# Where weight sums and weight staging stand among the reads of the product banks

## The chip, the core and the metric

The kernel runs on one core of a Trainium2 chip. The metric is the device time of one launch in microseconds (us). Three runs of the kernel before took 2848.87 to 2852.09 us, with a median of 2852.01 us.

## The reference, cut to what matters

The program is a small encoder trunk of two layers over 768 tokens (one request of 512, one of 256, weights shared), all in float32, model width 1024, inner width 2816:

```python
def swiglu_ffn(x, w1, w2):
    gate, up = jnp.split(x @ w1, 2, axis=-1)
    return (jax.nn.silu(gate) * up) @ w2
...
for li in range(DEPTH):
    x = x + 0.5 * swiglu_ffn(rmsnorm(x, norm_g[li, 0]), ffn_w1[li, 0], ffn_w2[li, 0])
    h = rmsnorm(x, norm_g[li, 1])
    ...  # layer 0: gated linear recurrence (HGRN2); layer 1: windowed attention
    x = x + mix
    x = x + 0.5 * swiglu_ffn(rmsnorm(x, norm_g[li, 2]), ffn_w1[li, 1], ffn_w2[li, 1])
return rmsnorm(x, final_norm_g)
```

There are four feed-forward networks (f0 to f3), and between them the HGRN2 mixer and the attention mixer. The change bears on the feed-forward networks above all.

## The kernel before

**Precision.** Each float32 operand is split into a rounded part ("hi", written by ScalarE as a cast to fp32r) and the rest ("lo", VectorE's subtraction). A product of two split operands is three matmuls: hi·hi, hi·lo, lo·hi.

**Seven products for eight.** The feed-forward products are cut into 2 by 2 blocks and done with a Winograd-style scheme of seven block products, p1 to p7, where some factors are sums of blocks. On the weights' side there are four sums: `s3` (a DRAM load to which GpSimd's DMA adds a block), `a21 += a22` (GpSimd's DMA adds one block to the other in SBUF), and two that VectorE forms: `a11 += a21` (call it the second sum; p6 reads it) and `a12 += a11` (the fourth sum; p3 reads it). p1 must read `a11` before the second sum overwrites it, and p2 must read `a12` before the fourth.

**One feed-forward network.** Its 22 inner blocks are worked in five groups g of four and a rest of two. For each inner block `up_pair` computes gate and up with seven products of twelve 128x384 matmuls (line 421), in the order p1 p7 p2 p5 p4 p6 p3, on four PSUM banks a to d; p2 is added onto the bank of p1, p4 onto that of p7, p3 onto that of p5, each after something has read the bank (lines 438 to 455). After four inner blocks `down_quad` multiplies the four hidden blocks by a 512x1024 piece of w2: seven products of eighteen 128x512 matmuls (line 479), in the order p1 p2 p5 p4 p7 p6 p3. Each product fills three banks (one for each block of 128 tokens), and VectorE reads each bank into the residual x with `add_x` (line 501). p2 goes onto the banks of p1, p4 onto those of p5, p3 onto those of p7, so a bank must have been read before the second of the pair writes to it. There are 20 such quads, five in each network. On TensorE the built order of a quad is p1, p2, p5, eight matmuls of p7, p4, the rest of p7, p6, p3.

**Staging of weights.** `load_next` issues a quad's raw loads on SyncE's queue into four `wr` buffers, and the DMAs that add blocks on GpSimd's. `quad_steps` gives one step for each product: `split` casts hi on ScalarE (line 199) and subtracts on VectorE (line 200; for p5 of an up pair on GpSimd), into eight `w` buffers. The steps p1 and p2 each add their sum right behind their split (lines 206 and 210). `done` frees a product's `w` buffers and calls `ahead`, which traces the next steps as far as buffers go. In the down quads a split covers 128x1024, in the up pairs 128x512.

**What sets the order.** The kernel is traced in Python, and a scheduler then sets each engine's instruction order from data dependences and priorities that follow the traced order. Each engine's queue runs strictly in the built order: an instruction that waits holds up all behind it. `keep_in_program_order` (new in the change) puts an instruction behind whatever was traced before it on its engine.

Of the kernel before, what the change touches and what calls it, by code (L numbers as in the profile page):

```python
# [23 lines left out]
NBLK = T // P  # L24
# [23 lines left out]
class Trunk:  # L48
# [123 lines left out]
    def quad_steps(self, key, raws, srcs, order):  # L172
        nc = self.nc
        flat = lambda t: t.rearrange("p a b -> p (a b)")
        up = len(raws) == 2
        if up:
            a11, a12, a21, a22 = (flat(t[:, h : h + 4, :]) for t in raws for h in (0, 4))
            three = [srcs[1].rearrange("(k p) c -> p k c", p=P)[:, :4, :]]
        else:
            a11, a12, a21, a22 = (flat(t) for t in raws)  # L180
            three = [srcs[2][:, i : i + 1, :] for i in range(2)]
        s3 = []
        for i, src in enumerate(three):
            t = self.wp.tile([P, 512], F32, tag="s3", name=self.name("s3"), bufs=2)
            self.last_load = nc.sync.dma_start(t.rearrange("p (a b) -> p a b", a=src.shape[1]), src)
            self.into(t, a11[:, i * 512 : (i + 1) * 512])
            s3.append(t)
        self.into(a21, a22)

        def split(name, srcs, eng=None):  # L190
            if up:
                w = self.wtile()
                hi, lo = w[:, :512], w[:, 512:]
            else:
                hi, lo = self.wtile(), self.wtile()
            n = srcs[0].shape[-1]
            for i, src in enumerate(srcs):
                h, l = (t[:, i * n : (i + 1) * n] for t in (hi, lo))
                nc.scalar.copy(h, src)  # L199
                (eng or nc.vector).tensor_sub(l, src, h.bitcast(F32))  # L200
            view = lambda t: t.rearrange("p (a b) -> p a b", a=4 if up else 2)
            self.staged[(*key, name)] = (view(hi), view(lo), 1 if up else 2)

        def p1():
            split("p1", [a11])
            nc.vector.tensor_add(a11, a11, a21)  # L206

        def p2():
            split("p2", [a12])
            nc.vector.tensor_add(a12, a12, a11)  # L210

        steps = {
            "p1": p1,
            "p2": p2,
            "p3": lambda: split("p3", [a12]),
            "p4": lambda: split("p4", [a22]),
            "p5": lambda: split("p5", [a21], nc.gpsimd if up else None),
            "p6": lambda: split("p6", [a11]),
            "p7": lambda: split("p7", s3),
        }  # L220
        return [(1 if up else 2, steps[name]) for name in order]

    def stage_next(self):
        if not self.loaded:
# [10 lines left out]
    def take(self, key):  # L235
        while key not in self.staged:
            self.stage_next()
        return self.staged[key][:2]

    def done(self, key):  # L240
        self.held -= self.staged.pop(key)[2]
        self.ahead()

    def ahead(self):
# [20 lines left out]
    def split(self, src, hi, lo):  # L265
        self.nc.scalar.copy(hi, src)  # L266
        self.nc.vector.tensor_sub(lo, src, hi.bitcast(F32))  # L267
# [148 lines left out]
    def product(self, key, name, src, ps, first, last):  # L416
        wh, wl = self.take((*key, name))
        for k in range(4):
            a, b = (wh[:, k, :], wl[:, k, :]), self.operand(src, k)
            for i, (x, y) in enumerate(((0, 0), (0, 1), (1, 0))):  # L420
                self.nc.tensor.matmul(  # L421
                    ps,
                    a[x],
                    b[y],
                    start=first and k == 0 and i == 0,
                    stop=k == 3 and i == 2,
                    skip_group_check=True,
                )
        self.done((*key, name))

    def up_pair(self, tag, j):
        nc = self.nc
        key = (tag, j)
        a, b, c, d = (self.ps(H) for _ in range(4))
        v, w, t = (self.tmp(H) for _ in range(3))
        p = lambda name, ps, first, last: self.product(key, name, FACTOR[name], ps, first, last)
        p("p1", a, True, False)
        nc.scalar.copy(v, a)
        p("p7", c, True, False)
        nc.scalar.copy(w, c)  # L440
        p("p2", a, False, True)
        nc.scalar.activation(a, a, AF.Silu)
        p("p5", d, True, False)
        nc.vector.tensor_sub(w, w, d)  # L444
        p("p4", c, False, True)
        p("p6", b, True, True)
        nc.vector.tensor_sub(v, v, b)
        nc.vector.tensor_sub(t, c, v)
        nc.vector.tensor_mul(t, t, a)  # L449
        yield t  # L450
        nc.vector.tensor_sub(w, w, v)
        p("p3", d, False, True)
        nc.vector.tensor_add(v, v, d)
        self.last_act = nc.scalar.activation(v, v, AF.Silu).ins
        self.last_dve = nc.vector.tensor_mul(w, v, w).ins
        yield w

    def down_quad(self, tag, g, hid):
        nc = self.nc
# [177 lines left out]
    def hgrn_proj(self, h, out):  # L637
        nc = self.nc
        qk = self.big([P, 2, T])
        qs, kd = qk[:, 0, :], qk[:, 1, :]  # L640
        f, q, k = (self.big([P, 2, T]) for _ in range(3))
        for c0, dst, func in ((0, qs, AF.Copy), (3, f[:, 1, :], AF.Sigmoid), (4, f[:, 0, :], AF.Sigmoid)):
            key = ("hgrn", h, c0)
            wh, wl = self.take(key)
            for s, (off, n) in enumerate(SEQS):
                ps = self.ps(n)
                for kk in range(NC):
                    b = tuple(self.h[kk][:, i, off : off + n] for i in range(2))
                    self.mm3(ps, (wh[:, kk, :], wl[:, kk, :]), b, kk == 0, kk == NC - 1)
                    if kk in ((1, 3, 5), (3,))[s]:  # L650
                        yield
                if s:
                    self.done(key)
                nc.scalar.activation(dst[:, off : off + n], ps, func)
                yield
        for d in range(2):
            fd, j = f[:, 1 - d, :], slice(h, h + 1)
            nc.vector.tensor_scalar(fd, fd, self.om_lb[:, d, j], self.lb[:, d, j], ALU.mult, ALU.add)
            nc.scalar.activation(k[:, d, :], fd, AF.Identity, bias=1.0, scale=-1.0)
            nc.vector.tensor_mul(q[:, 1 - d, :], qs, fd)  # L660
        nc.vector.tensor_add(kd, k[:, 0, :], k[:, 1, :])
        out.update(h=h, qs=qs, kd=kd, f=f, q=q, k=k)
# [340 lines left out]
    def out_proj(self, tag, half, act, next_row):  # L1003
        for c in range(2):
            for b in range(NBLK):
                ps = self.ps()
                sl = slice(b * P, (b + 1) * P)
                for i in range(4):
                    key = (tag, half, c, i // 2)
                    wh, wl = self.take(key)  # L1010
                    t = act[half * 4 + i]
                    self.mm3(ps, (t[:, 0, sl], t[:, 1, sl]), (wh[:, i % 2, :], wl[:, i % 2, :]), i == 0, i == 3)
                    if i % 2 and b == NBLK - 1:
                        self.done(key)
                    if i == 1:
                        yield
                self.add_x(self.x[b][:, c * 512 : (c + 1) * 512], ps, 1.0)
                if half and c:
                    self.after_block(b, next_row)
                    if b >= 4:  # L1020
                        self.run_later()
                elif not half and b % 2:
                    self.run_later()
                yield
# [257 lines left out]
```

## Time and profile before

| | |
|---|---|
| median of 3 runs | 2852.01 us |
| profiled execution | 2852.12 us, its span from first to last instruction 2850.3 us |
| TensorE clock granted | 0.998 |
| TensorE matmul busy | 2796.7 us, 98% of the span |
| VectorE busy | 2173.2 us, 76% |
| ScalarE busy | 1318.9 us, 46% |
| GpSimd busy | 355.1 us, 12% |
| DMA | mean 102 GB/s |

A row of the profile names the source line, the engine, the operation and the tiles as out<-in. PE is TensorE, DVE VectorE, ACT ScalarE, POOL GpSimd, SP SyncE. "Idle before" is how long the engine sat idle ahead of an instruction, and the arrow names what ended it. Matmuls are pipelined and their ends are modelled, so distances between starts say more than busy time.

### The profile page before, as it was taken

How to read it: one execution, taken by the hardware profiler on the slowest of the kernel's cores; microseconds unless marked ns; L12 is line 12 of the kernel's file. 1: busy time of each engine (PE TensorE's matmuls, PEld its weight loads, DVE VectorE, ACT ScalarE, POOL GpSimd, SP SyncE). 2: the span in 40 equal slices, each digit the busy share in tenths (PEclk: the TensorE clock that was granted, in tenths of full speed). 3: DMA queues.
4: the chain of work that ended last, by engine and by line, in shares of the span. 5: the costliest groups of instructions: out<-in, count | busy, mean ns of one | idle time of the engine just before them, and what ended most of it. 6: DMA issues, size and time to landing. Idle time of an engine off the chain costs nothing. (4 is left out here: it accounts for less than half of the span.)

```text
span 2850.3 us, 40558 instructions
## 1 busy us (share of the span) xinstructions
PE 2796.7 (98%) x15225; PEld 2554.2 (90%) x15225; DVE 2173.2 (76%) x3750; ACT 1318.9 (46%) x2454; POOL 355.1 (12%) x402
## 2 busy tenths in 40 slices
PE   8999999999999999999999999999999899999998
PEld 8899999889899889998998998999888789989997
DVE  7788787468577658878878887887848878788877
ACT  7344443434344336434444643444458755434443
POOL 1111111000000001111111111111002211111110
PEclk9999999999999999999999999999999999999999
DMA  6554454311111133555444355545422113555443
GB/s 165 127 125 122 116 134 121 115 44 39 44 39 38 60 97 86 132 127 122 123 119 114 84 134 127 122 121 124 126 71 75 37 51 90 135 126 125 117 121 96
DMA packets 330101, 291.37 MB, mean 102 GB/s; under 512 B 11608, under 2 KB 257840, under 8 KB 329904
## 3 DMA queue, kind: packets, MB, share of 16 engines
q1 hardware_dynamic: 294064, 212.43, 25.4%
q0 software_dynamic: 31680, 62.93, 12.6%
q10 hardware_dynamic: 4160, 13.42, 1.3%
q8 instruction: 119, 1.95, 0.3%
q14 instruction: 78, 0.64, 0.1%
HBM read 216.39 MB, written 9.44 MB: 79 GB/s over the span
## 5 line engine op out<-in xcount | busy, mean ns | idle before, releaser
L421 PE MATMUL ps<-big,w 128*128 128x384 f32 x6720 | 1172.8, 334 | 3.1 <-DVE tA L444 2.9
L421 PEld LDWEIGHTS ps<-big,w 128*128 128x128 f32 x6720 | 1165.4, 188 | 8.8 <-DVE tA L444 7.2
L199 ACT CAST w<-wr 128x512 fp32r<-128x512 f32 x600 | 416.1, 707 | 722.7 <-PE ps L421 321.0
L479 PE MATMUL ps<-w,big 128*128 128x512 f32 x2520 | 586.8, 391 | 17.4 <-DVE x L501 17.4
L479 PEld LDWEIGHTS ps<-w,big 128*128 128x128 f32 x2520 | 469.4, 188 | 129.7 <-DVE x L501 17.3
L200 DVE TENSOR_TENSOR w<-wr,w 128x512 fp32r<-128x512 f32 (+1 forms) x520 | 438.1, 853 | 95.7 <-ACT w L199 87.0
L501 DVE SCALAR_TENSOR_TENSOR x<-ps,x 128x512 f32<-128x512 f32 x468 | 305.5, 682 | 20.5 <-PE ps L479 10.2
L141 POOL DMA_DIRECT2D s<-wr x120 | 105.4, 878 | 1333.4 <-DMA wr<-in_ffn_w_dram 583.0
L261 PE MATMUL ps<-w,big 128*128 128x512 f32 x624 | 249.8, 400 | 0.2
L263 PE MATMUL ps<-w,big 128*128 128x512 f32 x624 | 245.2, 393 | 2.5 <-DVE big L330 1.3
L262 PE MATMUL ps<-w,big 128*128 128x512 f32 x624 | 244.4, 392 | 0.0
L266 ACT CAST big<-tA 128x384 fp32r<-128x384 f32 x296 | 148.0, 513 | 175.0 <-DVE tA L449 72.0
L261 PE MATMUL ps<-big,w 128*128 128x384 f32 (+2 forms) x640 | 220.8, 346 | 3.3 <-ACT big L266 2.0
L262 PE MATMUL ps<-big,w 128*128 128x384 f32 (+2 forms) x640 | 216.8, 339 | 0.7 <-DVE big L267 0.5
L263 PE MATMUL ps<-big,w 128*128 128x384 f32 (+2 forms) x640 | 215.7, 337 | 0.0
L167 DVE TENSOR_TENSOR w<-wr,w 128x1024 fp32r<-128x1024 f32 x92 | 111.6, 1222 | 83.6 <-ACT w L166 59.7
L141 POOL DMA_DIRECT2D wr<-wr x100 | 87.5, 875 | 680.0 <-DVE tA L350 319.8
L267 DVE TENSOR_TENSOR big<-tA,big 128x384 fp32r<-128x384 f32 x296 | 164.2, 566 | 7.9 <-ACT big L266 4.4
L206 DVE TENSOR_TENSOR wr<-wr,wr 128x512 f32<-128x512 f32 (+1 forms) x100 | 79.3, 793 | 114.5 <-DMA wr<-wr 85.9
L166 ACT CAST w<-wr 128x1024 fp32r<-128x1024 f32 x92 | 96.6, 1052 | 120.5 <-PE ps L262 99.7
L263 PEld LDWEIGHTS ps<-w,big 128*128 128x128 f32 x624 | 117.4, 188 | 28.8 <-DVE big L330 2.0
L261 PEld LDWEIGHTS ps<-w,big 128*128 128x128 f32 x624 | 117.8, 189 | 22.3 <-issue 0.6
(170 smaller groups left out, 3317.2 us busy)
## 6 DMA issues: line engine op xcount, KB each, us to landing
wr<-in_ffn_w_dram SPq DMA_DIRECT2D x264, 512.0 KB, 3.9
s<-in_ffn_w_dram SPq DMA_DIRECT2D x120, 256.0 KB, 3.0
s<-wr POOLq DMA_DIRECT2D x120, 256.0 KB, 4.0
wr<-wr POOLq DMA_DIRECT2D x80, 256.0 KB, 4.0
wr<-in_hg_w_in_dram SPq DMA_DIRECT2D x40, 512.0 KB, 3.8
wr<-wr POOLq DMA_DIRECT2D x20, 512.0 KB, 4.6
spill<-x ACTq DMA_DIRECT2D x12, 512.0 KB, 3.0
x<-spill ACTq DMA_DIRECT2D x12, 512.0 KB, 3.3
```

Source lines behind the costliest of these rows:

```text
L141: self.nc.gpsimd.dma_start(out, src, accum_op=ALU.add)
L167: self.nc.vector.tensor_sub(lo, raw, hi.bitcast(F32))
L199: nc.scalar.copy(h, src)
L200: (eng or nc.vector).tensor_sub(l, src, h.bitcast(F32))
L261: nc.tensor.matmul(out, a[0], b[0], start=first, stop=False)
L262: nc.tensor.matmul(out, a[0], b[1], start=False, stop=False)
L263: nc.tensor.matmul(out, a[1], b[0], start=False, stop=last)
L266: self.nc.scalar.copy(hi, src)
L267: self.nc.vector.tensor_sub(lo, src, hi.bitcast(F32))
L421: self.nc.tensor.matmul(ps, a[x], b[y], start=first and k == 0 and i == 0, stop=k == 3 and i == 2, skip_group_check=True,)
L479: nc.tensor.matmul(ps, a[x], w[y], start=name == chain and kp == 0 and q == 0, stop=kp == 1 and q == 2, skip_group_check=True,)
L501: self.nc.vector.scalar_tensor_tensor(x, ps, c, x, ALU.mult, ALU.add)
```

## The change

Three edits. First, the two VectorE sums of a weight quad leave the steps p1 and p2. In a down quad the second sum is traced right in front of the split of p6 and the fourth in front of that of p3; in an up pair the second sum follows the split of p5 and the fourth that of p4. Each is pinned behind what was traced before it on VectorE. Second, `product` no longer stages: it only releases its buffers, and `up_pair` calls `ahead` after the instruction that reads the product's bank. Third, in `hgrn_proj` and `out_proj` the call of `done` moves behind the read of the bank. No instruction is added or taken away but one activation-table load less on ScalarE.

```diff
@@ quad_steps
-        def p1():
-            split("p1", [a11])
-            nc.vector.tensor_add(a11, a11, a21)
-
-        def p2():
-            split("p2", [a12])
-            nc.vector.tensor_add(a12, a12, a11)
-
-        steps = {
-            "p1": p1,
-            "p2": p2,
-            "p3": lambda: split("p3", [a12]),
-            "p4": lambda: split("p4", [a22]),
-            "p5": lambda: split("p5", [a21], nc.gpsimd if up else None),
-            "p6": lambda: split("p6", [a11]),
-            "p7": lambda: split("p7", s3),
-        }
-        return [(1 if up else 2, steps[name]) for name in order]
+        own = {"p1": [a11], "p2": [a12], "p3": [a12], "p4": [a22], "p5": [a21], "p6": [a11], "p7": s3}
+        pin = self.tc.keep_in_program_order
+        add = {"second": lambda: nc.vector.tensor_add(a11, a11, a21), "fourth": lambda: nc.vector.tensor_add(a12, a12, a11)}
+        before = {} if up else {"p6": "second", "p3": "fourth"}
+        behind = {"p5": "second", "p4": "fourth"} if up else {}
+
+        def step(name):
+            if name in before:
+                pin(add[before[name]]())
+            split(name, own[name], nc.gpsimd if up and name == "p5" else None)
+            if name in behind:
+                pin(add[behind[name]]())
+
+        return [(1 if up else 2, lambda name=name: step(name)) for name in order]
@@
+    def release(self, key):
+        self.held -= self.staged.pop(key)[2]
+
     def done(self, key):
-        self.held -= self.staged.pop(key)[2]
+        self.release(key)
         self.ahead()
@@ product
-        self.done((*key, name))
+        self.release((*key, name))
@@ up_pair
         p("p1", a, True, False)
         nc.scalar.copy(v, a)
+        self.ahead()
         p("p7", c, True, False)
         nc.scalar.copy(w, c)
+        self.ahead()
         p("p2", a, False, True)
         nc.scalar.activation(a, a, AF.Silu)
+        self.ahead()
         p("p5", d, True, False)
         nc.vector.tensor_sub(w, w, d)
+        self.ahead()
         p("p4", c, False, True)
         p("p6", b, True, True)
         nc.vector.tensor_sub(v, v, b)
...
         nc.vector.tensor_sub(w, w, v)
+        self.ahead()
         p("p3", d, False, True)
...
         yield w
+        self.ahead()
@@ hgrn_proj
+                nc.scalar.activation(dst[:, off : off + n], ps, func)
                 if s:
                     self.done(key)
-                nc.scalar.activation(dst[:, off : off + n], ps, func)
@@ out_proj
-                    if i % 2 and b == NBLK - 1:
-                        self.done(key)
                     if i == 1:
+                        if b == NBLK - 1:
+                            self.done(key)
                         yield
                 self.add_x(self.x[b][:, c * 512 : (c + 1) * 512], ps, 1.0)
+                if b == NBLK - 1:
+                    self.done(key)
```

The order of instructions in the built programs shows what this moves. The three places below are of the same stretch, group 1 of f0: the end of the last up pair, the down quad, and the staging of the next group's weights. Line numbers of the changed kernel stand a few lines off: its 446, 450, 451, 452, 454, 457, 459 are 444, 447, 448, 449, 451, 453, 455 before, 506 is 501, 266 is 267, 349 is 350, and both sums stand on its line 206.

VectorE at the start of the quad, before. wr_224 to wr_227 are the quad's raw blocks a11, a12, a21, a22; w_239/w_240 are hi/lo of p2, w_241/w_242 of p5, w_243/w_244 of p4; ps_230 to ps_233 are the banks a to d of the up pair ahead.

```order
L206 TENSOR_TENSOR wr_224_1478<-wr_224_1478,wr_226_1482 128x1024
L200 TENSOR_TENSOR w_240_1565<-wr_225_1480,w_239_1564 128x1024
L444 TENSOR_TENSOR tA_235_1519<-tA_235_1519,ps_233_1517 128x384
L210 TENSOR_TENSOR wr_225_1480<-wr_225_1480,wr_224_1478 128x1024
L200 TENSOR_TENSOR w_242_1596<-wr_226_1482,w_241_1595 128x1024
L447 TENSOR_TENSOR tA_234_1518<-tA_234_1518,ps_231_1515 128x384
L448 TENSOR_TENSOR tA_236_1520<-ps_232_1516,tA_234_1518 128x384
L451 TENSOR_TENSOR tA_235_1519<-tA_235_1519,tA_234_1518 128x384
L449 TENSOR_TENSOR tA_236_1520<-tA_236_1520,ps_230_1514 128x384
L200 TENSOR_TENSOR w_244_1630<-wr_227_1484,w_243_1629 128x1024
L267 TENSOR_TENSOR big_204_1334<-tA_236_1520,big_204_1334 128x384
L453 TENSOR_TENSOR tA_234_1518<-tA_234_1518,ps_233_1517 128x384
```

The row behind these is the first read of one of the quad's banks (line 501). Now the changed kernel, where the last row shown is that first read:

```order
L200 TENSOR_TENSOR w_240_1565<-wr_225_1486,w_239_1564 128x1024
L446 TENSOR_TENSOR tA_235_1519<-tA_235_1519,ps_233_1517 128x384
L200 TENSOR_TENSOR w_242_1612<-wr_226_1488,w_241_1611 128x1024
L450 TENSOR_TENSOR tA_234_1518<-tA_234_1518,ps_231_1515 128x384
L451 TENSOR_TENSOR tA_236_1520<-ps_232_1516,tA_234_1518 128x384
L454 TENSOR_TENSOR tA_235_1519<-tA_235_1519,tA_234_1518 128x384
L452 TENSOR_TENSOR tA_236_1520<-tA_236_1520,ps_230_1514 128x384
L457 TENSOR_TENSOR tA_234_1518<-tA_234_1518,ps_233_1517 128x384
L200 TENSOR_TENSOR w_244_1633<-wr_227_1490,w_243_1632 128x1024
L266 TENSOR_TENSOR big_202_1328<-tA_236_1520,big_202_1328 128x384
L459 TENSOR_TENSOR tA_235_1519<-tA_234_1518,tA_235_1519 128x384
L506 SCALAR_TENSOR_TENSOR x_10_104<-ps_245_1648,x_10_104 128x512
```

Both sums of 128x1024 (lines 206 and 210) are gone from this stretch, and the read of bank d by line 457 now stands ahead of the split of p4.

VectorE later in the same quad, before. ps_245 to ps_247 are the banks of p1 and p2, ps_252 to ps_254 those of p5 and p4; w_250/w_251 belong to p6, w_255/w_256 to p3.

```order
L501 SCALAR_TENSOR_TENSOR x_5_94<-ps_245_1650,x_5_94 128x512
L501 SCALAR_TENSOR_TENSOR x_6_96<-ps_246_1658,x_6_96 128x512
L501 SCALAR_TENSOR_TENSOR x_7_98<-ps_247_1666,x_7_98 128x512
L200 TENSOR_TENSOR w_251_1702<-wr_224_1478,w_250_1701 128x1024
L501 SCALAR_TENSOR_TENSOR x_10_104<-ps_252_1705,x_10_104 128x512
L501 SCALAR_TENSOR_TENSOR x_11_106<-ps_253_1713,x_11_106 128x512
L501 SCALAR_TENSOR_TENSOR x_12_108<-ps_254_1721,x_12_108 128x512
L200 TENSOR_TENSOR w_256_1730<-wr_225_1480,w_255_1729 128x1024
L501 SCALAR_TENSOR_TENSOR x_5_94<-ps_252_1705,x_5_94 128x512
```

And the changed kernel:

```order
L506 SCALAR_TENSOR_TENSOR x_5_94<-ps_245_1648,x_5_94 128x512
L506 SCALAR_TENSOR_TENSOR x_6_96<-ps_246_1656,x_6_96 128x512
L506 SCALAR_TENSOR_TENSOR x_7_98<-ps_247_1664,x_7_98 128x512
L206 TENSOR_TENSOR wr_224_1484<-wr_224_1484,wr_226_1488 128x1024
L506 SCALAR_TENSOR_TENSOR x_10_104<-ps_252_1704,x_10_104 128x512
L506 SCALAR_TENSOR_TENSOR x_11_106<-ps_253_1712,x_11_106 128x512
L200 TENSOR_TENSOR w_251_1701<-wr_224_1484,w_250_1700 128x1024
L506 SCALAR_TENSOR_TENSOR x_12_108<-ps_254_1720,x_12_108 128x512
L206 TENSOR_TENSOR wr_225_1486<-wr_225_1486,wr_224_1484 128x1024
L506 SCALAR_TENSOR_TENSOR x_5_94<-ps_252_1704,x_5_94 128x512
L506 SCALAR_TENSOR_TENSOR x_6_96<-ps_253_1712,x_6_96 128x512
L200 TENSOR_TENSOR w_256_1730<-wr_225_1486,w_255_1729 128x1024
```

The second sum now stands between the reads of p2's banks and those of p5's, in the place of p6's split, which moves two rows back; the fourth sum stands ahead of p4's reads.

SyncE's queue of loads in the same stretch, before. wr_257, wr_258 and s3_259 belong to the first inner block of the next group (block 8), wr_260, wr_261 and s3_262 to block 9.

```order
L151 DMA wr_257_1733<-in_ffn_w1_dram 128x8x128
L151 DMA wr_258_1735<-in_ffn_w1_dram 128x8x128
L185 DMA s3_259_1737<-in_ffn_w1_dram 128x4x128
L185 DMA s3_262_1745<-in_ffn_w1_dram 128x4x128
L151 DMA wr_260_1741<-in_ffn_w1_dram 128x8x128
L151 DMA wr_261_1743<-in_ffn_w1_dram 128x8x128
```

And the changed kernel:

```order
L151 DMA wr_257_1733<-in_ffn_w1_dram 128x8x128
L185 DMA s3_259_1737<-in_ffn_w1_dram 128x4x128
L185 DMA s3_262_1745<-in_ffn_w1_dram 128x4x128
L151 DMA wr_258_1735<-in_ffn_w1_dram 128x8x128
L151 DMA wr_260_1741<-in_ffn_w1_dram 128x8x128
L151 DMA wr_261_1743<-in_ffn_w1_dram 128x8x128
```

The second raw load of block 8 (wr_258) moves behind both s3 loads, because its buffer is now the one of a21, which the moved second sum reads last.

## The prediction

> **What bounds the kernel now.** I read the page first, for how much of the span TensorE is idle.
>
> ```profile
> PE 2796.7 (98%) x15225; PEld 2554.2 (90%) x15225; DVE 2173.2 (76%) x3750; ACT 1318.9 (46%) x2454; POOL 355.1 (12%) x402
> L421 PE MATMUL ps<-big,w 128*128 128x384 f32 x6720 | 1172.8, 334 | 3.1 <-DVE tA L444 2.9
> L479 PE MATMUL ps<-w,big 128*128 128x512 f32 x2520 | 586.8, 391 | 17.4 <-DVE x L501 17.4
> ```
>
> TensorE is busy for 98% of the span, so only its idle time can be won: 2850.3 - 2796.7 = 53.6 us. The largest single piece of it stands before line 479, the down quads. Next the waits of TensorE, in us in total, times, longest:
>
> ```profile
> PE ps L479 <- DVE x L501: 17.4, 37, 0.5
> PE ps L421 <- DVE tA L444: 2.9, 5, 1.1
> ```
>
> Two kinds of wait bear on this change: matmuls of a down quad that wait for VectorE's read of a bank into x, 37 times in 20 quads, and matmuls of an up pair that wait for the read of bank d. Then TensorE in order of time over one quad (start, length, idle before):
>
> ```profile
> 173.97 4.28 PE L479 MATMUL ps<-w,big 128*128 128x512 f32 x18
> 178.77 10.26 PE L479 MATMUL ps<-w,big 128*128 128x512 f32 x44 [0.52 <-DVE x L501]
> 189.47 14.80 PE L479 MATMUL ps<-w,big 128*128 128x512 f32 x64 [0.45 <-DVE x L501]
> 204.11 2.09 PE L421 MATMUL ps<-big,w 128*128 128x384 f32 x11
> ```
>
> The last 64 matmuls run undisturbed: (204.11 - 189.47) / 64 = 0.229 us each. At that pace the first 18 take 4.12 us and the next 44 take 10.07; they took 4.80 and 10.70. So a quad loses 0.68 us ahead of p2 and 0.63 us ahead of p4, which goes onto p5's banks. What VectorE did in the meantime (idle before in brackets):
>
> ```profile
> 168.88 1.22 DVE L206 TENSOR_TENSOR wr<-wr,wr 128x1024 f32<-128x1024 f32 x1 [5.94 <-issue]
> 170.02 1.22 DVE L200 TENSOR_TENSOR w<-wr,w 128x1024 fp32r<-128x1024 f32 x1
> 171.15 0.55 DVE L444 TENSOR_TENSOR tA<-tA,ps 128x384 f32<-128x384 f32 x1
> 171.62 1.22 DVE L210 TENSOR_TENSOR wr<-wr,wr 128x1024 f32<-128x1024 f32 x1
> 172.75 1.22 DVE L200 TENSOR_TENSOR w<-wr,w 128x1024 fp32r<-128x1024 f32 x1
> 173.89 0.54 DVE L447 TENSOR_TENSOR tA<-tA,ps 128x384 f32<-128x384 f32 x1
> 174.47 0.56 DVE L448 TENSOR_TENSOR tA<-ps,tA 128x384 f32<-128x384 f32 x1
> ...
> 175.87 1.22 DVE L200 TENSOR_TENSOR w<-wr,w 128x1024 fp32r<-128x1024 f32 x1
> 177.01 0.55 DVE L267 TENSOR_TENSOR big<-tA,big 128x384 fp32r<-128x384 f32 x1
> 177.48 0.55 DVE L453 TENSOR_TENSOR tA<-tA,ps 128x384 f32<-128x384 f32 x1
> 177.94 0.68 DVE L501 SCALAR_TENSOR_TENSOR x<-ps,x 128x512 f32<-128x512 f32 x1
> 178.61 0.56 DVE L455 TENSOR_TENSOR tA<-tA,tA 128x384 f32<-128x384 f32 x1
> 179.09 0.68 DVE L501 SCALAR_TENSOR_TENSOR x<-ps,x 128x512 f32<-128x512 f32 x1
> ...
> 180.23 0.68 DVE L501 SCALAR_TENSOR_TENSOR x<-ps,x 128x512 f32<-128x512 f32 x1
> 180.83 0.55 DVE L350 TENSOR_TENSOR tA<-tA,tA 128x384 f32<-128x384 f32 x1
> 181.29 0.69 DVE L200 TENSOR_TENSOR w<-s,w 128x512 fp32r<-128x512 f32 x1
> ...
> 184.71 0.68 DVE L200 TENSOR_TENSOR w<-s,w 128x512 fp32r<-128x512 f32 x1
> 185.33 0.56 DVE L267 TENSOR_TENSOR big<-tA,big 128x384 fp32r<-128x384 f32 x1
> 185.81 1.88 DVE L501 SCALAR_TENSOR_TENSOR x<-ps,x 128x512 f32<-128x512 f32 x3
> 187.60 1.21 DVE L200 TENSOR_TENSOR w<-wr,w 128x1024 fp32r<-128x1024 f32 x1
> 188.74 1.88 DVE L501 SCALAR_TENSOR_TENSOR x<-ps,x 128x512 f32<-128x512 f32 x3
> ```
>
> VectorE sat idle for 5.94 us in front of the second sum (line 206), then ran almost without a pause to the end of the rows. The first read of p1's bank began at 177.94, although its six matmuls were through at 173.97 + 6 x 0.229 = 175.34. The queue is late, not the data. It is late because the second sum waited, with everything behind it:
>
> ```profile
> 168.85 1.05 ACT L199 CAST w<-wr 128x1024 fp32r<-128x1024 f32 x1 [2.90 <-DMA wr<-wr]
> ```
>
> ScalarE's cast of p5 started in the same moment on the landing of `a21 += a22`, which the second sum also reads.
>
> **The change, part by part.** Starts of neighbours give what a VectorE row costs in a full queue: a 1024-wide row 1.14 us (170.02 - 168.88), a 384-wide one 0.47 (177.94 - 177.48 is 0.46), a read of a bank 0.60.
>
> *Sums out of the quad's start.* Walk VectorE's queue in the new order of this quad. The split of p2 and line 446 (444 before) no longer stand behind the landing. p5's split follows the cast, at 169.9 to 171.0. Line 450 waits for the end of the up pair's p6, and 451, 454, 452 follow; all are done when p3 ends near 174.2. From there: line 457 at 174.2, p4's split 174.7, lines 266 and 459 at 175.8 and 176.3, the first read at 176.75, released at 177.4. TensorE wants that bank at 173.97 + 4.12 = 178.09: 0.7 us to spare. The second and third reads come at 177.95 and 179.0, wanted 1.37 and 2.75 us after 178.09. The first bubble goes.
>
> *Sum put in front of p6's split.* From the third read at 179.0 the new order runs 0.60 for the read, seven 384-wide rows and two 512-wide splits of p7. Before, the ten rows from 180.83 to 185.81 took 4.98; now line 349 stands ahead of the third read and the rest takes about 4.5, so p2's three reads start at 184.1. The second sum follows at 185.9, the first read of p5's banks at 187.05, released at 187.75. TensorE wants it after 62 matmuls, at 173.97 + 62 x 0.229 = 188.17. It is 0.4 us early, less 0.05 to 0.15 us for the hand-over (178.62 to 178.77 before). The second bubble goes too, with little to spare. The cast of p6 now waits for the sum, until 187.2, and that of p3 until 191.3; TensorE wants these products after 90 and 108 matmuls, at 194.6 and 198.7, so their extra wait costs nothing.
>
> *Reads ahead of staging in the up pairs.* The reads of a to d move ahead of casts and splits, and the sums of 512 move two places back. Cover: the read of d (446) has 24 matmuls of line 421 between p5's end and p3, 24 x 0.174 = 4.2 us by the 11 matmuls in 2.09 us above, less the last one's 0.33, against 0.55 for itself and 0.7 for the sum now in front of it. Cost nothing. What goes are the 5 waits for line 444, which the landing ahead of the quad made.
>
> *The moved load.* The second raw load of the next block now waits for the second sum, until 187.1 (before: until p4's split), behind both s3 loads on SyncE and behind one more of GpSimd's DMAs. Its times, from issue to landing:
>
> ```profile
> wr<-in_ffn_w_dram SPq DMA_DIRECT2D x264, 512.0 KB, 3.9
> wr<-wr POOLq DMA_DIRECT2D x80, 256.0 KB, 4.0
> 195.70 0.68 DVE L206 TENSOR_TENSOR wr<-wr,wr 128x512 f32<-128x512 f32 x1
> ```
>
> 187.1 + 3.9 + 0.9 for GpSimd's issue + 4.0 = 195.9. VectorE's queue in the new order reaches the next block's second sum near 197.8 (four 1024-wide rows, nine reads and three 512-wide splits after 185.9, 11.8 us at the prices above). So it does not wait there. Behind that sum stand the reads of p6's and p3's banks; GpSimd's p5 split, now ahead of a DMA in its queue, is wanted only some 13 us later.
>
> *hgrn_proj, out_proj, the attention's edges.* There the change swaps a cast with a read of a bank, the order of a few matmuls at the attention's first projection, and one load of an activation table less at the HGRN2's start.
>
> ```profile
> 464.00:1066.00 602.00, 599.65 (x3567) 534.01 (x3566) 391.42 (x682) 237.24 (x407) 4.88 (x5) 1.00 0.21 63
> 2063.00:2342.00 279.00, 268.51 (x1440) 221.85 (x1439) 196.08 (x567) 187.40 (x483) 53.03 (x98) 0.99 0.19 58
> ```
>
> TensorE is busy for 599.65 of 602.00 us in the HGRN2 stretch and 268.51 of 279.00 in the attention's. A gain is at most 2.4 and 10.5 us; a loss, by the longest single wait above (1.1 us) at two or three edges, some 3. Nearest is nothing, since the rows there are hardly reordered: 0, with -3 to +3 for the range.
>
> *Sum.* 20 second bubbles x 0.63 = 12.6; 37 - 20 = 17 first bubbles x 0.68 = 11.6; the waits for line 444, where idle time understates the loss as above (0.63 against 0.45), 2.9 + 5 x 0.18 = 3.8. Together 28.0 us. The bounds: 17.4 + 2.9 = 20.3 if only the listed idle time comes back, and 20 x 1.31 + 3.8 + 3 = 33 if all quads lose both and the mixers gain. The profiled execution took 2852.12 us and the median is 2852.01, the same. 2852.1 - 28.0 = 2824; since waits below the listing's sight would go as well, I take 2823.
>
> **The rivals.**
>
> *The second bubble stays in part.* The 0.3 us to spare ahead of p4 is the thinnest place of the walk. If the walk is late by 0.8 us, TensorE still waits 0.5 in each of 20 quads: 10 us less, 2833. For it: the rows run one behind another with three hand-overs to ScalarE in between. Against: even then p4 starts earlier than before.
>
> *The bubble is the banks'.* The mechanism would be that a product cannot follow on its own bank in time whatever VectorE's order is, so it only changes its releaser: 2852, no change. The Trainium skill's page Perfetto Trace Analysis (Optimization Strategy) says that a gap repeating on the engine that should be saturated can mean too few buffers, SBUF or PSUM; this change adds none. Against it: the bank was ready to be read at 175.34, a read takes 0.68, and it was wanted at 178.09.
>
> *The load comes too late (slower).* If the next block's `a21` lands after 197.8, VectorE stands still, with six reads behind it. Banks are taken in turn, so the next pair's bank c is p3's first, wanted at 202.8 + 2.1 = 204.9; from the landing to the end of its read stand the sum, four reads, two splits, the fourth sum and a cast, some 5.6 us, so it decides from a landing at 199.3 on. With both DMAs at twice their medians the landing is at 203.8 and each quad loses 4.5 us: 20 x 4.5 - 28 = 62 us slower, 2914. For it: the load, its queue places and GpSimd's order all move back. Against: 195.9 leaves 3.4 us.
>
> **How the numbers follow.** Both bubbles gone 0.70 (2817 to 2831, between the sum's bounds of 33 and 20.3 us); second in part 0.17 (2831 to 2838); no change 0.07; late load or another new wait that makes it slower 0.06. The range 2816 to 2838 holds the first two, 0.87 before what falls off their ends. A measurement of this kernel can tell about 0.2%, 5.7 us, from no change: faster 0.87, same 0.07, slower 0.06.
>
> **What would show it.** The waits of line 479's successor for the read into x should fall from 17.4 us to under 3, and the row for line 444 should vanish; a quad's 126 matmuls should take 28.9 us, not 30.1; no 5.94 us of idle VectorE ahead of a 1024-wide sum. I am wrong if TensorE waits ahead of p4 in most quads, or if VectorE's 512-wide second sum of the first block after a quad waits for a DMA.

## The result and the profile after

Shared runs of both kernels: 2851.95 us before (2848.87 to 2852.09, 4 runs), 2815.46 us changed (2814.95 to 2816.13, 4 runs), ratio 0.9875 with a 95% interval of 0.9858 to 0.9892. That is 36.5 us less; the forecast was 29 less. The profiled execution took 2815.21 us, its span is 2813.4 us, the granted clock 0.998 as before. The times below are of runs at a granted clock of 0.996 or more; one of the ten runs of e2 had 0.85, took 3060.27 us and is left out.

The page of the changed kernel, engines and the two groups of matmuls (behind the bar: busy us, mean ns | idle us ahead of them and what ended it):

```profile
PE 2781.1 (99%) x15225; PEld 2557.6 (91%) x15225; DVE 2162.5 (77%) x3750; ACT 1324.6 (47%) x2453; POOL 366.5 (13%) x402
L420 PE MATMUL ps<-big,w 128*128 128x384 f32 x6720 | 1169.2, 334 | 0.0
L484 PE MATMUL ps<-w,big 128*128 128x512 f32 x2520 | 575.3, 389 | 0.0
```

Add busy and idle of a line, and compare with before. The down quads took 586.8 + 17.4 = 604.2 us and take 575.3: 28.9 less. The up pairs took 1172.8 + 3.1 = 1175.9 and take 1169.2: 6.7 less. Together 35.6 of the span's 2850.3 - 2813.4 = 36.9. Over two fifths of it were never listed as idle: the busy time of the same matmuls fell too, by 11.5 and 3.6 us.

The waits of TensorE, longest sums first (us in total, times, longest). Neither the down quads' line (484) nor the up pairs' (420) is in this list any more:

```profile
PE ps L111 <- DMA tB<-in_hg_g_norm_dram: 7.5, 1, 7.5
PE ps L915 <- DVE big L266: 3.1, 3, 1.9
PE ps L1113 <- ACT tA L1104: 2.5, 6, 1.3
```

The quad that the prediction walked through (f0 group 1), TensorE in order of time:

```profile
170.58 28.76 PE L484 MATMUL ps<-w,big 128*128 128x512 f32 x126
199.18 7.99 PE L420 MATMUL ps<-big,w 128*128 128x384 f32 x45
```

One unbroken row of 126 matmuls: 199.18 - 170.58 = 28.60 us, 0.227 each, where it was three rows and 30.14 us. Below, T0 is the start of a quad's first matmul, here 170.58. VectorE in the same quad (rows in between left out):

```profile
171.25 1.22 DVE L200 TENSOR_TENSOR w<-wr,w 128x1024 fp32r<-128x1024 f32 x1
...
173.32 0.68 DVE L506 SCALAR_TENSOR_TENSOR x<-ps,x 128x512 f32<-128x512 f32 x1
...
175.53 0.69 DVE L506 SCALAR_TENSOR_TENSOR x<-ps,x 128x512 f32<-128x512 f32 x1
...
180.62 1.88 DVE L506 SCALAR_TENSOR_TENSOR x<-ps,x 128x512 f32<-128x512 f32 x3
182.41 1.22 DVE L206 TENSOR_TENSOR wr<-wr,wr 128x1024 f32<-128x1024 f32 x1
183.54 1.28 DVE L506 SCALAR_TENSOR_TENSOR x<-ps,x 128x512 f32<-128x512 f32 x2
...
195.11 0.69 DVE L206 TENSOR_TENSOR wr<-wr,wr 128x512 f32<-128x512 f32 x1 [0.68 <-DVE w L200]
```

The first read of p1's banks starts at T0+2.74 (before: 177.94 - 173.97 = 3.97), the first of p5's at T0+12.96 (before: 188.74, T0+14.77). What VectorE waits for at its second sums, before (here the 128x1024 ones of the down quads):

```profile
DVE wr L206 <- DMA wr<-wr: 85.9, 15, 6.8
DVE wr L206 <- issue: 28.0, 5, 5.9
```

and after (here the 128x512 ones of up pairs; ahead of the forty 128x1024 sums VectorE is idle for 0.0 us):

```profile
DVE wr L206 <- issue: 15.9, 11, 1.8
DVE wr L206 <- DVE w L200: 1.8, 3, 0.7
```

The 113.9 us in 20 waits, one for each quad, are gone. What is left, 17.7 us in 14 waits of at most 1.8 us, stands at another place: at the second sum of the up block staged behind a quad, which before had 0.6 us of idle time in all.

### The profile page after: what moved, and what is told of

Its sections match the earlier page's. It is cut to its first block, busy times and chain, and to the rows that moved or that the text cites. A ratio compares the mean times of both kernels' runs of the same rounds, so it can differ in the third digit from the quotient of the medians.

```text
span 2813.4 us, 40558 instructions
## 1 busy us (share of the span) xinstructions
PE 2781.1 (99%) x15225; PEld 2557.6 (91%) x15225; DVE 2162.5 (77%) x3750; ACT 1324.6 (47%) x2453; POOL 366.5 (13%) x402
## 3 DMA queue, kind: packets, MB, share of 16 engines
q8 instruction: 119, 1.95, 0.3%
## 4 chain that ended last, share of the span: by engine, by line
PE 95%; ACT 2%; DVE 2%; POOL 0%; issue 0%; DMA 0%; DVEq 0%; SPq 0%; ACTq 0%; POOLq 0%
PE ps L420 41%; PE ps L484 20%; PE ps L262 8%; PE ps L261 8%; PE ps L260 8%; PE ps L676 3%; PE ps L770 1%; PE ps L322 1%; PE ps L746 1%; PE ps L1151 1%; ACT big L1129 0%; PE ps L1113 0%; PE ps L1164 0%; PE ps L1114 0%; PE ps L915 0%; PE ps L1163 0%
## 5 line engine op out<-in xcount | busy, mean ns | idle before, releaser
L420 PE MATMUL ps<-big,w 128*128 128x384 f32 x6720 | 1169.2, 334 | 0.0
L484 PE MATMUL ps<-w,big 128*128 128x512 f32 x2520 | 575.3, 389 | 0.0
L484 PEld LDWEIGHTS ps<-w,big 128*128 128x128 f32 x2520 | 472.7, 188 | 97.5
L200 POOL TENSOR_TENSOR w<-wr,w 128x512 fp32r<-128x512 f32 x80 | 131.4, 1643 | 195.5 <-ACT w L199 195.5
L262 PEld LDWEIGHTS ps<-w,big 128*128 128x128 f32 x624 | 117.2, 188 | 28.3 <-DVE big L989 2.0
L206 DVE TENSOR_TENSOR wr<-wr,wr 128x512 f32<-128x512 f32 (+1 forms) x120 | 125.3, 1044 | 17.8 <-issue 15.9
```

Source lines behind the costliest of these rows:

```text
L206: add = {"second": lambda: nc.vector.tensor_add(a11, a11, a21), "fourth": lambda: nc.vector.tensor_add(a12, a12, a11)}
L262: nc.tensor.matmul(out, a[1], b[0], start=False, stop=last)
L420: self.nc.tensor.matmul(ps, a[x], b[y], start=first and k == 0 and i == 0, stop=k == 3 and i == 2, skip_group_check=True,)
L484: nc.tensor.matmul(ps, a[x], w[y], start=name == chain and kp == 0 and q == 0, stop=kp == 1 and q == 2, skip_group_check=True,)
```

## The experiments

The theory (queue theory): in each quad VectorE stood at the second sum until the landing of `a21 += a22`, and all reads of banks behind it came late; where the down sums stand is the whole effect. Rivals: the staging calls do it; the sums' own work does it; the bubble is the banks'. Each kernel ran beside the kernel before, which had medians of 2851.8 to 2853.2 us in the three sessions.

**Down sums alone (e1).** Into the kernel before, only this:

```diff
-            nc.vector.tensor_add(a11, a11, a21)
+            if up:
+                nc.vector.tensor_add(a11, a11, a21)
...
+        def p6():
+            if not up:
+                pin(nc.vector.tensor_add(a11, a11, a21))
+            split("p6", [a11])
```

and the same for the fourth sum in front of p3's split.

> Kernel before, with only the two VectorE sums of the down quads moved and pinned (in front of the splits of p6 and p3); the up pairs' sums, the staging, hgrn_proj and out_proj as before. Theory Q (the losses come from VectorE's queue, which at the start of a down quad stands behind the second sum and its wait for the landing of a21 += a22): all of line 479's loss and line 444's waits go, 2816 us within 4. Theory S (the gain comes from reading the banks ahead of staging in the up pairs): the sums' place matters little, 2845 to 2852.

Measured: 2821.0 us (2819.27 to 2822.14), ratio 0.9891 (0.9876 to 0.9906): 32 of the 36.5 us, and 1 us above what the theory gave. Its groups:

```profile
L435 PE MATMUL ps<-big,w 128*128 128x384 f32 x6720 | 1169.2, 334 | 0.0
L493 PE MATMUL ps<-w,big 128*128 128x512 f32 x2520 | 577.5, 390 | 2.1 <-DVE x L515 1.3
```

The up pairs are already where the changed kernel has them, so their waits came from the down sums too. The down quads keep 577.5 + 2.1 - 575.3 = 4.3 us too much. Most of it lies ahead of p3, worst in this quad (TensorE, then VectorE):

```profile
1705.79 24.68 PE L493 MATMUL ps<-w,big 128*128 128x512 f32 x108
1731.50 4.37 PE L493 MATMUL ps<-w,big 128*128 128x512 f32 x18 [1.03 <-DVE x L515]
```

```profile
1730.07 0.69 DVE L209 TENSOR_TENSOR wr<-wr,wr 128x512 f32<-128x512 f32 x1 [2.68 <-issue]
1730.67 1.88 DVE L515 SCALAR_TENSOR_TENSOR x<-ps,x 128x512 f32<-128x512 f32 x3
```

The same fault one block later: the next up block's second sum (here still in step p1, line 209) waits 2.68 us, and the reads of p7's banks, which p3 goes onto, stand behind it.

**All sums, no staging edits (e11).** The whole first hunk of the change in the kernel before, nothing else:

```diff
+        before = {} if up else {"p6": "second", "p3": "fourth"}
+        behind = {"p5": "second", "p4": "fourth"} if up else {}
```

> The kernel before with all sums moved (those of the up blocks too) and none of the other edits: the staging calls, the decay projections and the output projections stand as before. With the down sums alone moved the time was 2821.0, with the staging alone 2849.5. Left there was a stall of 0.4 to 1.2 us at p3's first matmul in 8 of 20 quads, and in it the second sum of the next up block stood ahead of the tail reads of p7's banks and waited for its landing. Sum theory: with that sum behind p5 as well the stall goes, and the time is that of the changed kernel, 2814 to 2818; the staging edits are worth nothing. Rival (staging is what takes away the rest): 2820 to 2823, with the stall at p3 still in the down quads.

Measured: 2816.92 us (2816.74 to 2817.21), ratio 0.9875 (0.9862 to 0.9889). Its down quads:

```profile
L475 PE MATMUL ps<-w,big 128*128 128x512 f32 x2520 | 575.3, 389 | 0.0
```

It is the changed kernel's time within what can be told. The up sums' place is worth e1's remaining 4 us.

**Staging calls alone (e2).**

```diff
@@ product
-        self.done((*key, name))
+        self.release((*key, name))
@@ up_pair, after each read of a bank
+        self.ahead()
```

> Changed kernel with the old quad steps (sums right behind the splits of p1 and p2) and the old hgrn_proj and out_proj: only the staging in the up pairs is behind the reads. Theory Q: the queue still stands behind the second sum at a quad's start, 2848 to 2852, with about 37 waits of TensorE for the reads into x as before. Theory S: 2815 to 2822.

Measured: 2849.2 us (2847.65 to 2852.56), ratio 0.9989 (0.9979 to 0.9998), so at most some 6 us less. The wait is all there, only gathered into the first bubble: 20 waits in place of 37.

```profile
PE ps L488 <- DVE x L510: 17.9, 20, 1.0
```

**Projections alone (e4).** Only the hunks of `hgrn_proj` and `out_proj`:

```diff
+                nc.scalar.activation(dst[:, off : off + n], ps, func)
                 if s:
                     self.done(key)
-                nc.scalar.activation(dst[:, off : off + n], ps, func)
```

> The kernel before with only the edits of the decay and the output projections: the staging call behind the read of the bank. The prediction took 0 plus or minus 3 us for these: 2849 to 2855. A rival that puts the undersized part of the forecast (8 us) here: 2843 to 2846.

Measured: 2851.18 us, ratio 0.9997 (0.9988 to 1.0005): nothing.

**The changed kernel without the pin (e8).**

```diff
-        pin = self.tc.keep_in_program_order
+        pin = lambda ins: ins
```

> Changed kernel without the pins: the sums are traced at their new places, but nothing holds them there, and the built order puts both down-quad sums back to the start of the quad. Theory Q: no gain, 2848 to 2852, both bubbles of a quad back. If the place in the traced source were enough: 2815.

Measured: 2851.16 us, ratio 0.9995 (0.9985 to 1.0004), and the old wait under its new line:

```profile
PE ps L484 <- DVE x L506: 17.6, 19, 1.0
```

In the built order both sums are back at the quad's start. The second sum in the quad of f0 group 1:

```profile
171.28 1.23 DVE L206 TENSOR_TENSOR wr<-wr,wr 128x1024 f32<-128x1024 f32 x1 [5.82 <-issue]
```

So the pin carries the gain, not the place in the source. That the scheduler puts them there because it takes the landing to be earlier than it is would explain it; only the order was seen.

**The fourth sum alone (e10).** As e1, but the second sum stays in step p1:

```diff
+        def p3():
+            if not up:
+                pin(nc.vector.tensor_add(a12, a12, a11))
+            split("p3", [a12])
```

> Kernel before with only the fourth sum of the down quads moved and pinned (in front of p3's split); the second sum keeps its place and its wait for the landing. Theory Q, by the walk of VectorE's queue in the quad shown: everything behind the fourth sum comes 1.14 us earlier, so the first bubble (0.7 us) goes, of the second about 0.15 us a quad stays (3 us in all), and the waits ahead of an up pair's p3 (6.6 us) stay: 2851.9 - 26 = 2826 us. A theory in which each sum's 1.14 us of work costs half of the bubbles gives 2834; one in which the landing alone costs gives 2848 to 2852.

Measured: 2832.18 us (2828.52 to 2833.54), ratio 0.9928 (0.9911 to 0.9944), between the 2826 and the 2834 that had been priced. Its groups:

```profile
L432 PE MATMUL ps<-big,w 128*128 128x384 f32 x6720 | 1173.4, 335 | 3.9 <-DVE tA L455 3.9
L490 PE MATMUL ps<-w,big 128*128 128x512 f32 x2520 | 581.0, 391 | 2.0
```

Against the changed kernel the down quads keep 581.0 + 2.0 - 575.3 = 7.7 us where 3 had been expected, and the up pairs 1173.4 + 3.9 - 1169.2 = 8.1 where it was 6.6. The quad of f0 group 1 (TensorE; then VectorE's sum and its first reads of p1's and p5's banks):

```profile
172.35 29.24 PE L490 MATMUL ps<-w,big 128*128 128x512 f32 x126
201.43 3.83 PE L432 MATMUL ps<-big,w 128*128 128x384 f32 x21
```

```profile
167.28 1.23 DVE L208 TENSOR_TENSOR wr<-wr,wr 128x1024 f32<-128x1024 f32 x1 [5.82 <-issue]
175.21 0.69 DVE L512 SCALAR_TENSOR_TENSOR x<-ps,x 128x512 f32<-128x512 f32 x1
186.02 1.88 DVE L512 SCALAR_TENSOR_TENSOR x<-ps,x 128x512 f32<-128x512 f32 x3
```

The wait of 5.82 us is untouched, but with 1.14 us less work behind it the first read starts at T0+2.86 and the first bubble goes. p5's first read ends at 186.02 + 0.68 - 172.35 = T0+14.35; TensorE wants the bank after 62 matmuls at T0+14.07. Part of the second bubble stays: the quad takes 29.08 us, 0.48 more than in the changed kernel. So the first bubble here needed both, the late landing and the fourth sum's 1.14 us behind it; part of the second bubble and the waits of the up pairs stay without that work.

**Take only the wait away (e5).** The kernel before, both sums where they were; in the down blocks the second sum adds a22, which lands earlier than the a21 that the DMA adds it into (so p6's right factor is another matrix):

```diff
-            nc.vector.tensor_add(a11, a11, a21)
+            nc.vector.tensor_add(a11, a11, a21 if up else a22)
```

> The kernel before; in the down blocks alone the second sum adds the fourth raw block, which has landed long before, in place of the third, into which the last transfer adds (so p6's right factor is another matrix: part of the computation is changed). The two sums stay where they were, at the start of the quad, and take VectorE 1.4 us there, but wait for no landing. Queue theory (VectorE stands still at the second sum until the landing, with the reads of the banks behind it): both bubbles and the waits at line 444 go, 2815 to 2820. Rival (work: the sums' own time ahead of the reads is what delays p4 and p2): 2840 to 2852, since only the wait is gone and the work is all there.

Measured: 2816.35 us (2814.93 to 2818.09), ratio 0.9873 (0.986 to 0.9887). VectorE's waits at the sum, and the groups:

```profile
DVE wr L206 <- DMA wr<-in_ffn_w_dram: 8.1, 16, 0.8
```

```profile
L421 PE MATMUL ps<-big,w 128*128 128x384 f32 x6720 | 1169.2, 334 | 0.0
L479 PE MATMUL ps<-w,big 128*128 128x512 f32 x2520 | 575.9, 390 | 0.0
```

The same sums in the same place, the same banks, and the gain of the whole change: 2851.89 - 2816.35 = 35.5 us, though the sum still waits up to 0.8 us for the load of a22 ("long before" in the expectation was too much said). This settles it: the wait for one landing, with the queue behind it, cost those 35.5 us. That the sums' work is enough by itself is out, and so is "the bubble is the banks'".

**More work at the quad's start (e6).** In the changed kernel:

```diff
                 (eng or nc.vector).tensor_sub(l, src, h.bitcast(F32))
+                if not up and name in ("p5", "p4"):
+                    nc.vector.tensor_sub(l, src, h.bitcast(F32))
```

> The changed kernel with the subtraction of the low part done twice for p5 and for p4 of the down quads (the second writes the same values): two times 1.14 us more work of VectorE ahead of the reads of the banks. By the walk in the prediction the last read of p1's banks has 0.4 us to spare and p2's reads still less: the first bubble comes back at about 1.9 us a quad and another 1.7 us ahead of p2's third block, 20 quads times 3.6 = +72, 2888 (taken for a range: 2850 to 2890). If VectorE's queue at the start of a quad isn't what the matmuls wait for: 2814 to 2818.

Measured: 2823.11 us (2821.25 to 2825.81), ratio 0.9897 (0.9881 to 0.9912); neither forecast. The quad of f0 group 1, TensorE and VectorE's first read of p1's banks:

```profile
174.37 28.84 PE L486 MATMUL ps<-w,big 128*128 128x512 f32 x126
```

```profile
179.06 0.68 DVE L508 SCALAR_TENSOR_TENSOR x<-ps,x 128x512 f32<-128x512 f32 x1
```

The read did come 1.95 us later (T0+4.69), but the scheduler built another order of TensorE too: six matmuls of p5 now stand ahead of p2, so the bank is wanted six matmuls later, at T0 + 24 x 0.227 = T0+5.45, and the read ends at T0+5.37. The experiment doesn't test the walk in the changed kernel's order. Here six other matmuls cover the added work; that the scheduler put them there because it saw that work is likely, and not shown. The cover isn't complete: e6 is 7.6 us slower than the changed kernel, and by the page of its profile 578.2 + 1.8 - 575.3 = 4.7 us of that lie in the down quads.

**A later landing (e12).** To move the landing without moving any instruction, the changed kernel with one more accumulation in the 20 up blocks that follow a quad (so their weights hold a21 + 2 a22):

```diff
-        self.into(a21, a22)
+        for _ in range(2 if up and key[-1] % 4 == 0 and key[-1] else 1): self.into(a21, a22)
```

> The changed kernel, but for the 20 up blocks that follow a quad GpSimd's DMA adds a22 into a21 twice, one after the other (so these weights are wrong: a21 + 2 a22). The built order of every engine is word for word that of the changed kernel, with only those 20 DMAs added; what moves is the landing that the next block's second sum waits for, from T0+24.45 in the quad of f0 group 1 to some 4.0 to 5.2 us later (one more DMA from issue to landing), T0+28.5 to 29.6. The prediction's third rival had put the point from which a late landing costs TensorE at T0+25.3. If that holds: 3.2 to 4.3 us in each of 20 quads, 64 to 86 us, 2880 to 2901, with a stall at the first matmul onto p3's bank in the next up pair. If there is more cover than that (in the changed kernel the sum already waits up to 1.8 us without a stall): 2815 to 2825.

Measured: 2844.18 us (2840.33 to 2846.72), ratio 0.9974 (0.9963 to 0.9985). 28.7 us of the gain are lost again, less than the 64 to 86 that the decision point had given. The waits (VectorE; TensorE), then f0 group 1 (TensorE; VectorE's sum; ScalarE):

```profile
DVE wr L206 <- issue: 93.6, 20, 5.5
```

```profile
PE ps L420 <- ACT tA L437: 20.5, 15, 1.7
```

```profile
172.19 28.76 PE L484 MATMUL ps<-w,big 128*128 128x512 f32 x126
200.79 4.35 PE L420 MATMUL ps<-big,w 128*128 128x384 f32 x24
206.42 8.76 PE L420 MATMUL ps<-big,w 128*128 128x384 f32 x49 [1.28 <-ACT tA L437]
```

```profile
201.07 0.69 DVE L206 TENSOR_TENSOR wr<-wr,wr 128x512 f32<-128x512 f32 x1 [5.03 <-issue]
```

```profile
204.85 1.14 ACT L199 CAST w<-wr 128x512 fp32r<-128x512 f32 x2 [2.04 <-DVE wr L206]
205.90 0.47 ACT L437 COPY tA<-ps 128x384 f32<-128x384 f32 x1
```

Here the sum starts at 201.07, T0+28.88, 4.35 us later than in the changed kernel. The quad itself is undisturbed, and the next pair's p1 and p7 (24 matmuls) run. p2 then waits for ScalarE's copy of bank a (line 437), which stands behind two casts that wait for VectorE's sums. 24 matmuls of 0.174 us end at 204.97, the next starts at 206.42: 1.45 us lost. The list has 15 such waits, not 20; by the page of its profile the up pairs take 1173.8 + 20.5 - 1169.2 = 25.1 us more, and its profiled execution, 2840.67 us, is 25.5 us slower than the changed kernel's. As an estimate from this one quad, TensorE begins to lose when the sum starts after T0 + 28.88 - 1.45 = T0+27.4, not 25.3, and by another chain: ScalarE's queue, not the reads of p3's banks. The changed kernel agrees: its longest wait, 1.8 us at 2756.90, puts a sum at T0+25.6, and the up pairs show no loss.

**p5's split of the up pairs on VectorE (e13).** The changed kernel with:

```diff
-            split(name, own[name], nc.gpsimd if up and name == "p5" else None)
+            split(name, own[name], None)
```

> The changed kernel with p5's subtraction of the up pairs on VectorE too, 80 rows of about 0.69 us more there (+55 us busy) and none of it on GpSimd. In the changed kernel the 512-wide sums of line 206 took 958 ns in the mean, 685 before. If GpSimd's subtraction at the same time is what slows them: the mean falls to 680 to 700, and so does the longest, from 2.5 us to under 0.8. If not (a landing, the place of the sum): it stays above 850. The time: VectorE is at 77%, and up pairs lost nothing to it in the changed kernel, so 2815 to 2822 if the extra rows find idle time, more if they stand ahead of reads.

Measured: 2816.61 us (2815.8 to 2817.05), ratio 0.9876 (0.9861 to 0.9892); the changed kernel's time. What it shows of the engines stands in the last section.

## Why the prediction was right, and where its sizes were off

- *What bounds it, and the sums moved out of the quad's start.* Right. The walk gave the first read at T0+2.78, p2's reads at T0+10.1, the second sum at T0+11.9 and p5's first read at T0+13.1; the rows have T0+2.74, 10.04, 11.83 and 12.96. e5 shows the cause by itself.
- *Second bubble 12.6 and first bubbles 11.6: mis-sized.* Their sum of 24.2 us measured 28.9. The pace of 0.229 us was taken from the quad's last 64 matmuls, which held 0.1 us of loss themselves; undisturbed it is 28.60 / 126 = 0.227. With it the first 18 matmuls and the next 44 each lost 0.71 us in that quad, not 0.68 and 0.63, and the quad as a whole 1.54, not 1.31. The count of 17 first bubbles was not the error: 28.9 us are 1.45 a quad in the mean, less than 1.54, so some quads did lose less.
- *Waits for line 444, 3.8: mis-sized.* It measured 6.7, by e1 from the down sums alone. The list named 5 waits; the busy time of line 421 held another 3.6 us.
- *The upper bound of 33 was none*, since it used the same pace and the same 3.8. With the measured terms it would be 20 x 1.54 + 6.7 = 37.5. The range's low end came from this bound, and the measured median, 2815.46, lies 0.5 us below it.
- *Reads ahead of staging: cost nothing, gain nothing.* Right where it counts: e2 alone came to 2849.2, by its interval 0.6 to 6 us less, but e11 has the changed kernel's time without them. *Projections, 0 with -3 to +3:* e4, 0.7 us less, within its interval of no change.
- *The moved load.* VectorE reached the next block's second sum at 195.11 - 0.68 = T0+23.85 (walk: T0+23.8). The load was issued at T0+13.08 (walk: 13.1), but from there to GpSimd's accumulating DMA it took 189.85 - 183.66 = 6.2 us where the walk had the median's 3.9, and from there to the sum 5.3 (walk: 4.9). So the sum did wait, 0.68 us here and up to 1.8. Its row names VectorE's own split, but that ended at 194.43; the trace has the landing of GpSimd's DMA at 195.03, and e12 moved the sum by moving the landing alone. "So it does not wait there" was wrong, and one of the signs by which the prediction would have called itself wrong, a 512-wide second sum behind a quad that waits for a DMA, did come. It cost nothing, since by the estimate from e12 27.4 - 24.5 = 2.9 us of cover were left. SyncE's and GpSimd's rows of the changed kernel:

```profile
183.66 6.98 SPq L151 DMA_DIRECT2D wr<-in_ffn_w_dram  x3
```

```profile
189.85 0.87 POOL L141 DMA_DIRECT2D wr<-wr  x1 [5.72 <-DMA wr<-in_ffn_w_dram]
```

- *Rival, the second bubble stays in part:* seen in e10, where the read is released 0.7 us later; in the changed kernel it ended at 183.54 + 0.68 = T0+13.64 against T0+14.07 wanted. *Rival, the banks':* out by e5; the cause that the Trainium skill's page Perfetto Trace Analysis (Optimization Strategy) names as possible for a repeating gap, too few buffers, was not the cause of this one. *Rival, the late load:* its mechanism is real; its decision point was 2.1 us too early, by that estimate, and its place wrong.

## What to carry to other kernels

An instruction that waits for a transfer, on an in-order queue ahead of reads that free PSUM banks, costs TensorE the time by which the reads come after it wants those banks; look at what stands behind the instruction, not at its own 1.2 us. Move it behind those reads and pin it there: left free, the scheduler put it back (e8). Take an undisturbed pace from a stretch known to be free of waits, and compare two kernels by busy plus idle time of whole groups: idle time alone showed 20.5 of 35.6 us here.

## What the runs showed of the hardware

VectorE's 512-wide second sums got slower in the changed kernel, 958 ns in the mean where they took 685. Their groups before, then after:

```profile
L206 DVE TENSOR_TENSOR wr<-wr,wr 128x512 f32<-128x512 f32 x80 | 54.8, 685 | 0.6
```

```profile
L206 DVE TENSOR_TENSOR wr<-wr,wr 128x512 f32<-128x512 f32 x80 | 76.6, 958 | 17.8 <-issue 15.9 <-DVE w L200 1.8
```

One such sum, and GpSimd's subtraction in the middle of it:

```profile
149.04 2.50 DVE L206 TENSOR_TENSOR wr<-wr,wr 128x512 f32<-128x512 f32 x1
149.37 1.62 POOL L200 TENSOR_TENSOR w<-wr,w 128x512 fp32r<-128x512 f32 x1
```

The sum ends 0.55 us after GpSimd's row ends. With that subtraction on VectorE (e13) these sums take 684 ns; their group, all 512-wide subtractions of line 200, and the engines:

```profile
L206 DVE TENSOR_TENSOR wr<-wr,wr 128x512 f32<-128x512 f32 x80 | 54.7, 684 | 0.0
L200 DVE TENSOR_TENSOR w<-wr,w 128x512 fp32r<-128x512 f32 x480 | 327.4, 688 | 135.0 <-ACT w L199 127.3
```

```profile
PE 2781.6 (99%) x15225; PEld 2558.2 (91%) x15225; DVE 2169.4 (77%) x3830; ACT 1325.0 (47%) x2453; POOL 244.5 (9%) x322
```

VectorE then does 80 rows of 0.688 us more, 55 us, and is busy only 2169.4 - 2162.5 = 6.9 us longer: GpSimd's help had cost VectorE some 48 us. The Trainium skill's page SBUF — State Buffer (Who interferes with whom) says that a VectorE instruction with two SBUF inputs contends with a GpSimd instruction that reads SBUF, through a shared port pair; these rows agree. Here neither place costs time, since no matmul waits for those sums.
